# Moving seven-product operand preparation earlier in a Strassen feed-forward

## The chip, the cores and the metric

One NeuronCore of a Trainium2 chip runs the whole program. The metric is the device time of one execution in microseconds (us), lower is better.

## The reference, cut to what matters

The program computes a hybrid decoder in f32: two layers with a squared-ReLU feed-forward, then a block with a gated feed-forward. Only the three feed-forwards touch this change.

```python
def _mlp(x, w_up, w_down):                     # twice: DEPTH = 2, D_MODEL 1024, D_FF 4096, 512 tokens
    h = jax.nn.relu(x @ w_up)
    return (h * h) @ w_down
...
        gate = causal_dwconv3(h @ w_gate[i], ffn_conv_w[i], ffn_conv_b[i])      # D_FF_2 2816
        x = x + (jax.nn.silu(gate) * (h @ w_up[i])) @ w_down[i]
```

## The kernel before, in words

Every f32 matmul is done as three fp32r matmuls of 128x128 by 128x512 (`mm3`, L202 to L204): high by high, high by low, low by high. An operand is therefore split first: ScalarE (ACT) casts the high part (L119), VectorE (DVE) subtracts it to get the low part (L120). TensorE (PE) takes both.

**Up parts.** The hidden features are made in "parts" of 256 columns: two PSUM banks, 48 matmuls, two weight chunks (`wchunk`, or `pair_of` in the gated block) that are loaded by SP, then split on ACT and DVE into one of four `wh`/`wl` buffers. In the two MLPs a part is evacuated by ACT (ReLU, L1003, square, L1008). In the gated block a gate part `gp` goes through a convolution (L1310, L1311, L1313) and SiLU (L1582), and an up part `up` is multiplied in on DVE, into `hr` (L1592) or, for groups 8 to 10, into `a` (L1597) and split again into `ah`, `al`.

**Strassen steps.** The product with the down weights is done, for 1024 hidden columns at a time, as seven products of 24 matmuls each (`down_steps`, a generator that yields after each product). It runs three times per MLP and twice in the gated block (c = 0, 1). The feature side comes from two raw tiles `hr` with quarters A11, A21 (`ra`) and A12, A22 (`rb`). `a_op` copies a quarter into a split tile `aop` (one ACT cast, one DVE subtraction), `a_sum` (L910) forms a sum of quarters in place on DVE. The weight side comes from four tiles `wq`: `b_sum` (L916, DVE) and `b_op`. The products, with their feature operand: 1 a11; 2 s3 = A11 - A21; 3 s2 = A22 - A21'; 4 a12; 5 s1 = A11 + A22'; 6 a22, copied before A22 is overwritten; 7 s4 = A12 - A22'. `add` (L880) adds finished banks `r` into the residual on DVE.

**What sets the order.** A scheduler orders each engine's queue by the order in which the code is written, less a head start: operand and sum instructions have 120 places (`A_PRIO`), weight splits 80 or 60. Each engine then runs its queue strictly in that order. In the MLPs the mix is product 1, 2, 3, part, 4, part, 5, 6, part, 7, part (`WEAVE`); in the gated block one product and one part alternate, gate and up in turn, so that product 3 of c = 0 stands between the up part of group 4 and the gate part of group 5, and product 3 of c = 1 between the up part of group 8 and the gate part of group 9. There are 13 tiles for operands, features and inputs (`bp`) and 8 PSUM banks, of which the products hold up to six.

`tc.issue_after(ins)` orders, of the instructions written inside it, those on the engine of `ins` behind `ins` in that engine's queue.

Of the kernel before, what the change touches and what calls it, by code (L numbers as in the profile page):

```python
# [14 lines left out]
AF = mybir.ActivationFunctionType  # L15
ALU = mybir.AluOpType
# [30 lines left out]
A_PRIO, B_PRIO = 120, 80  # L47
# [4 lines left out]
def tile_hybrid_decoder(ctx: ExitStack, tc: tile.TileContext, io: dict, out: bass.AP):  # L52
    nc = tc.nc
# [9 lines left out]
    def pool(name, bufs, side=None):  # L63
        return tc.tile_pool(name=name, bufs=bufs, side=side, reuse_waits="tile")
# [3 lines left out]
    def big(name, dt=F32R):  # L68
        n_big[0] += 1
        return bp.tile([P, 4, S], dt, tag="b", name=f"{name}_{n_big[0]}")  # L70

    def bank(name="pb"):
        n_big[0] += 1
        return ps.tile([P, S], F32, tag="ps", name=f"{name}_{n_big[0]}")

    def small(n, name):
        n_big[0] += 1
        return sm.tile([P, n], F32, tag=f"s{n}", name=f"{name}_{n_big[0]}")
# [14 lines left out]
    turned = {}  # L93
# [24 lines left out]
    def split(hi, lo, src, src2=None):  # L118
        turned["hi"] = nc.scalar.copy(out=hi, in_=src).ins  # L119
        return nc.vector.tensor_tensor(out=lo, in0=src, in1=hi.bitcast(F32), op=ALU.subtract)  # L120
# [79 lines left out]
    def mm3(o, st, mv, start, stop):  # L200
        (sh, sl), (mh, ml) = st, mv
        nc.tensor.matmul(o, lhsT=sh, rhs=mh, start=start, stop=False, skip_group_check=True)  # L202
        nc.tensor.matmul(o, lhsT=sh, rhs=ml, start=False, stop=False, skip_group_check=True)  # L203
        nc.tensor.matmul(o, lhsT=sl, rhs=mh, start=False, stop=stop, skip_group_check=True)  # L204
# [43 lines left out]
    def krows(W, k0, kn, c0, n):  # L248
        return W[k0 * P:(k0 + kn) * P, c0:c0 + n].rearrange("(k p) c -> p k c", p=P)
# [203 lines left out]
    class Norm:  # L453
# [5 lines left out]
        def add(self, gi, t, pb, alpha):  # L459
            if t not in self.sums:  # L460
                self.sums[t] = small(2, "sum")
            cs = slice(gi * 512, gi * 512 + 512)
            nc.vector.scalar_tensor_tensor(out=self.x[:, t, cs], in0=self.x[:, t, cs], scalar=alpha, in1=pb,
                                           op0=ALU.mult, op1=ALU.add, accum_out=self.sums[t][:, gi:gi + 1])
# [412 lines left out]
    def ev_add(x, alpha):  # L877
        def ev(gi, t, pb):
            cs = slice(gi * 512, gi * 512 + 512)
            nc.vector.scalar_tensor_tensor(out=x[:, t, cs], in0=x[:, t, cs], scalar=alpha, in1=pb,  # L880
                                           op0=ALU.mult, op1=ALU.add)
        return ev
# [2 lines left out]

    ts2 = slice(0, 256), slice(256, 512)

    def down_steps(mb, wd, row, ra, rb, alpha):


        A11, A21, A12, A22 = ra[:, :, ts2[0]], ra[:, :, ts2[1]], rb[:, :, ts2[0]], rb[:, :, ts2[1]]
        B = {}
        for r, h in ((0, 0), (1, 1), (0, 1), (1, 0)):
            n_big[0] += 1
            B[r, h] = q = mb.tile([P, 4, S], F32, tag="q", name=f"wq_{n_big[0]}")
            for i in range(2):
                nc.sync.dma_start(out=q[:, 2 * i:2 * i + 2, :],
                                  in_=krows(wd, row + r * 4 + 2 * i, 2, h * 512, 512))
        B11, B12, B21, B22 = B[0, 0], B[0, 1], B[1, 0], B[1, 1]

        def a_op(src):
            o = big("aop")
            hl = o.rearrange("p k c -> p (k c)").rearrange("p (f k c) -> p f k c", f=2, k=4)
            with tc.high_priority(offset=A_PRIO):
                split(hl[:, 0], hl[:, 1], src)
            return hl

        def a_sum(out, a, b, op):
            with tc.high_priority(offset=A_PRIO):
                nc.vector.tensor_tensor(out=out, in0=a, in1=b, op=op)  # L910

        def b_sum(out, a, b, op):
            with tc.high_priority(offset=A_PRIO):
                for i in range(2):
                    ks = slice(2 * i, 2 * i + 2)
                    nc.vector.tensor_tensor(out=out[:, ks, :], in0=a[:, ks, :], in1=b[:, ks, :], op=op)  # L916

        def b_op(src):
            res = []
            for i in range(2):  # L920
                n_big[0] += 1
                wh = wp.tile([P, 1024], F32R, tag="wh", name=f"wh_{n_big[0]}")
                wl = wp.tile([P, 1024], F32R, tag="wl", name=f"wl_{n_big[0]}")
                with tc.high_priority(offset=B_PRIO):
                    split(wh, wl, src[:, 2 * i:2 * i + 2, :].rearrange("p k c -> p (k c)"))
                res.append([t.rearrange("p (k c) -> p k c", k=2) for t in (wh, wl)])
            return res

        def product(R, a, b, start):
            for i, (wh, wl) in enumerate(b):  # L930
                for tb in range(2):
                    for k in range(2):
                        ts_ = slice(tb * P, (tb + 1) * P)
                        kk = 2 * i + k
                        mm3(R[tb], (a[:, 0, kk, ts_], a[:, 1, kk, ts_]), (wh[:, k, :], wl[:, k, :]),
                            start and kk == 0, kk == 3)

        def add(R, th, h, al=1.0):
            for tb in range(2):
                ev_add(x, al)(h, 2 * th + tb, R[tb])  # L940

        def banks2(n):
            return [bank(n) for _ in range(2)]

        a11 = a_op(A11)
        b = b_op(B11)
        R1 = banks2("r")
        product(R1, a11, b, True)
        for th, h in ((0, 1), (1, 0), (1, 1)):
            add(R1, th, h, alpha)  # L950
        yield
        a_sum(A21, A11, A21, ALU.subtract)
        s3 = a_op(A21)
        b_sum(B12, B22, B12, ALU.subtract)
        b = b_op(B12)
        R3 = banks2("r")
        product(R3, s3, b, True)
        add(R3, 1, 1)
        yield
        a22 = a_op(A22)  # L960
        a_sum(A22, A22, A21, ALU.subtract)
        s2 = a_op(A22)
        b_sum(B11, B12, B11, ALU.add)
        b = b_op(B11)
        R2 = banks2("r")
        product(R2, s2, b, True)
        add(R2, 1, 0)
        yield
        a12 = a_op(A12)
        b = b_op(B21)  # L970
        product(R1, a12, b, False)
        add(R1, 0, 0, alpha)
        yield
        a_sum(A11, A11, A22, ALU.add)
        s1 = a_op(A11)
        b_sum(B21, B21, B11, ALU.subtract)
        b_sum(B11, B22, B11, ALU.subtract)
        b = b_op(B11)
        product(R2, s1, b, False)
        add(R2, 1, 1)  # L980
        yield
        b = b_op(B21)
        product(R3, a22, b, False)
        add(R3, 1, 0)
        yield
        a_sum(A12, A12, A22, ALU.subtract)
        s4 = a_op(A12)
        b = b_op(B22)
        product(R2, s4, b, False)
        add(R2, 0, 1)  # L990
        yield
# [316 lines left out]
    def conv3(y, u, wi, nm, m, bi):  # L1308

        nc.scalar.activation(y, u, AF.Identity, scale=col(wi + 2 * nm + m), bias=col(bi + m))  # L1310
        nc.vector.scalar_tensor_tensor(out=y[:, 1:], in0=u[:, :S - 1], scalar=col(wi + nm + m), in1=y[:, 1:],  # L1311
                                       op0=ALU.mult, op1=ALU.add)
        nc.vector.scalar_tensor_tensor(out=y[:, 2:], in0=u[:, :S - 2], scalar=col(wi + m), in1=y[:, 2:],  # L1313
                                       op0=ALU.mult, op1=ALU.add)
# [245 lines left out]
    wg, wu, wd = io["w_gate_2"][0], io["w_up_2"][0], io["w_down_2"][0]  # L1560
    with pool("ff", 2) as ff:
        H = []

        RAW = {}
# [12 lines left out]
        def gate_ev(gr, banks):  # L1577
            for m in range(2):
                n_big[0] += 1
                Y[gr, m] = y = ff.tile([P, S], F32, tag="y", name=f"y_{n_big[0]}")  # L1580
                conv3(y, banks[m], V_FW, 22, gr * 2 + m, V_FB)
                nc.scalar.activation(y, y, AF.Silu)  # L1582

        def up_ev(gr, banks):
            if gr < 8 and gr % 2 == 0:
# [58 lines left out]
                gated(gr, part)  # L1644
        with pool("fb", 4) as fb:
            for c in range(2):
                ds = down_steps(fb, wd, c * 8, RAW.pop(2 * c), RAW.pop(2 * c + 1), 1.0)
                for gr in range(4 * c + 4, min(4 * c + 8, 11)):
                    for part in range(2):
                        next(ds, None)  # L1650
                        gated(gr, part)
                for _ in ds:
                    pass
# [100 lines left out]
```

## Time and profile before

| what | value |
|---|---|
| time, median of 3 runs (lowest, highest) | 1725.74 us (1725.26, 1726.1) |
| the profiled execution's own time | 1721.95 us |
| its span, first to last instruction | 1720.2 us |
| PE busy, share of the span | 1679.5 us, 98% |
| DVE busy | 1109.6 us, 65% |
| ACT busy | 827.4 us, 48% |
| mean granted TensorE clock | 0.991 of full speed |

The profile is of one execution. A busy matmul of 389 ns overlaps the next one, so the pace of PE is read from the distance between starts. A timeline row gives start, length, engine, line, operation, output<-inputs, how many were merged, and in brackets the idle time before it with what ended it.

### The profile page before, as it was taken

Reading aid. Unit: us, or ns where it says so; the run is one execution under the profiler, and the core shown is the slowest. Engines: PE = TensorE matmul, PEld = TensorE weight load, DVE = VectorE, ACT = ScalarE, POOL = GpSimd, SP = SyncE. Lnnn points to the kernel's source line nnn. Section 1 sums busy time; section 2 is a strip of 40 time slices with the busy share of each in tenths; the row PEclk is TensorE's granted clock in tenths of the full one; section 3 lists DMA queues with packets and bytes.
Section 4 is the critical chain, followed back from the end, with each engine's and each line's share of the span. In section 5 each row is a group of like instructions: output and inputs, shape, how many; then the busy total and the mean of one; then the engine's idle time right before and its main releaser. Section 6 shows DMA issues by size and latency. Waiting matters only on the chain.

```text
span 1720.2 us, 21303 instructions
## 1 busy us (share of the span) xinstructions
PE 1679.5 (98%) x8239; PEld 1388.6 (81%) x8239; DVE 1109.6 (65%) x1938; ACT 827.4 (48%) x1415; POOL 8.0 (0%) x10
## 2 busy tenths in 40 slices
PE   8799999999999999999999999999999999999999
PEld 8577898888888877798888888988778878878887
DVE  5577558685845678747576846556765567667553
ACT  4366445444543578444444545444853333434442
POOL 0000000000000000000000000001000000000000
PEclk9899999999999999999999999999999999999999
DMA  5722442423132323413333133132352223321331
GB/s 183 107 66 79 142 147 62 134 74 123 49 111 86 105 69 113 158 50 98 98 98 98 49 128 107 40 132 86 100 183 62 86 86 92 117 63 60 99 97 62
DMA packets 128087, 167.57 MB, mean 97 GB/s; under 512 B 9049, under 2 KB 84082, under 8 KB 127986
## 3 DMA queue, kind: packets, MB, share of 16 engines
q1 hardware_dynamic: 119072, 150.03, 28.0%
q10 hardware_dynamic: 8914, 16.18, 3.9%
q8 instruction: 65, 1.06, 0.3%
q14 instruction: 36, 0.29, 0.1%
HBM read 160.95 MB, written 5.24 MB: 97 GB/s over the span
## 4 chain that ended last, share of the span: by engine, by line
PE 92%; DVE 3%; DMA 2%; ACT 2%; ACTq 1%; issue 0%; SPq 0%; DVEq 0%
PE up L203 8%; PE up L202 8%; PE up L204 8%; PE r L204 6%; PE r L202 6%; PE r L203 6%; PE tt L203 3%; PE tt L204 3%; PE tt L202 3%; PE tm L202 2%; PE tm L204 2%; PE fm L202 2%; PE tm L203 2%; PE fm L203 2%; PE fm L204 2%; PE gp L202 2%
## 5 line engine op out<-in xcount | busy, mean ns | idle before, releaser
L120 DVE TENSOR_TENSOR wl<-wr,wh 128x1024 fp32r<-128x1024 f32 (+5 forms) x219 | 223.0, 1031 | 183.0 <-ACT wh L119 182.2
L119 ACT CAST wh<-wr 128x1024 fp32r<-128x1024 f32 (+5 forms) x219 | 193.5, 898 | 285.2 <-PE up L203 112.5
L203 PE MATMUL up<-xtl,wh 128*128 128x512 f32 x608 | 236.5, 389 | 0.0
L202 PE MATMUL up<-xth,wh 128*128 128x512 f32 x608 | 236.5, 389 | 0.0
L204 PE MATMUL up<-xth,wl 128*128 128x512 f32 x608 | 236.2, 389 | 0.0
L120 DVE TENSOR_TENSOR wl<-wq,wh 128x1024 fp32r<-128x1024 f32 x112 | 136.8, 1222 | 109.5 <-ACT wh L119 109.5
L119 ACT CAST wh<-wq 128x1024 fp32r<-128x1024 f32 x112 | 118.1, 1054 | 172.4 <-PE r L204 94.0
L202 PE MATMUL r<-wh,aop 128*128 128x512 f32 x448 | 175.8, 392 | 6.2 <-ACT aop L119 6.2
L203 PE MATMUL r<-wl,aop 128*128 128x512 f32 x448 | 175.4, 392 | 0.0
L204 PE MATMUL r<-wh,aop 128*128 128x512 f32 x448 | 174.3, 395 | 0.0
L204 PEld LDWEIGHTS up<-xth,wl 128*128 128x128 f32 x608 | 114.1, 188 | 23.7
L203 PEld LDWEIGHTS up<-xtl,wh 128*128 128x128 f32 x608 | 114.1, 188 | 23.6
L202 PEld LDWEIGHTS up<-xth,wh 128*128 128x128 f32 x608 | 114.1, 188 | 23.6
L202 PEld LDWEIGHTS r<-wh,aop 128*128 128x128 f32 x448 | 84.8, 189 | 24.7 <-ACT aop L119 7.5
L204 PEld LDWEIGHTS r<-wh,aop 128*128 128x128 f32 x448 | 84.6, 189 | 21.6 <-DVE aop L120 4.2
L203 PEld LDWEIGHTS r<-wl,aop 128*128 128x128 f32 x448 | 84.7, 189 | 17.8
L880 DVE SCALAR_TENSOR_TENSOR x<-x,r 128x512 f32<-128x512 f32 x144 | 92.3, 681 | 1.2 <-PE r L204 1.2
L120 DVE TENSOR_TENSOR aop<-hr,aop 128x1024 fp32r<-128x1024 f32 x56 | 67.1, 1221 | 24.5 <-ACT aop L119 24.5
L916 DVE TENSOR_TENSOR wq<-wq,wq 128x1024 f32<-128x1024 f32 x64 | 76.3, 1219 | 5.2 <-DMA wq<-in_w_down_dram 4.1
L203 PE MATMUL gp<-xtl,wh 128*128 128x512 f32 x160 | 62.3, 389 | 0.0
L202 PE MATMUL gp<-xth,wh 128*128 128x512 f32 x160 | 62.3, 389 | 0.0
L204 PE MATMUL gp<-xth,wl 128*128 128x512 f32 x160 | 62.2, 389 | 0.0
(423 smaller groups left out, 3552.9 us busy)
## 6 DMA issues: line engine op xcount, KB each, us to landing
wr<-in_mlp_w_up_dram SPq DMA_DIRECT2D x64, 512.0 KB, 3.8
wq<-in_mlp_w_down_dram SPq DMA_DIRECT2D x48, 512.0 KB, 4.8
wr<-in_w_in_dram SPq DMA_DIRECT2D x24, 512.0 KB, 4.9
wr<-in_w_gate_dram SPq DMA_DIRECT2D x22, 512.0 KB, 3.6
wr<-in_w_up_dram SPq DMA_DIRECT2D x22, 512.0 KB, 3.7
wr<-in_mlp_w_down_dram SPq DMA_DIRECT2D x16, 512.0 KB, 3.8
wq<-in_w_down_dram SPq DMA_DIRECT2D x16, 512.0 KB, 4.0
wr<-in_mla_w_o_dram SPq DMA_DIRECT2D x8, 512.0 KB, 3.7
```

What stands on the lines that cost most here:

```text
L119: turned["hi"] = nc.scalar.copy(out=hi, in_=src).ins
L120: return nc.vector.tensor_tensor(out=lo, in0=src, in1=hi.bitcast(F32), op=ALU.subtract)
L202: nc.tensor.matmul(o, lhsT=sh, rhs=mh, start=start, stop=False, skip_group_check=True)
L203: nc.tensor.matmul(o, lhsT=sh, rhs=ml, start=False, stop=False, skip_group_check=True)
L204: nc.tensor.matmul(o, lhsT=sl, rhs=mh, start=False, stop=stop, skip_group_check=True)
L880: nc.vector.scalar_tensor_tensor(out=x[:, t, cs], in0=x[:, t, cs], scalar=alpha, in1=pb, op0=ALU.mult, op1=ALU.add)
L916: nc.vector.tensor_tensor(out=out[:, ks, :], in0=a[:, ks, :], in1=b[:, ks, :], op=op)
```

## The change

In `down_steps`, the sum and the split of a product's feature operand are written one product earlier: behind the matmuls of the product before and ahead of that product's `add` and `yield`, so ahead of the part that follows the `yield`. In the gated block the generator also gets the last SiLU instruction traced so far, and the `b_sum` instructions are written inside `tc.issue_after` of it. The diff:

```diff
-    def down_steps(mb, wd, row, ra, rb, alpha):
+    def down_steps(mb, wd, row, ra, rb, alpha, after=None):
...
         def b_sum(out, a, b, op):
-            with tc.high_priority(offset=A_PRIO):
+            with ExitStack() as es:
+                es.enter_context(tc.high_priority(offset=A_PRIO))
+                if after:
+                    es.enter_context(tc.issue_after(after))
...
         product(R1, a11, b, True)
+        a_sum(A21, A11, A21, ALU.subtract)
+        s3 = a_op(A21)
         for th, h in ((0, 1), (1, 0), (1, 1)):
             add(R1, th, h, alpha)
         yield
-        a_sum(A21, A11, A21, ALU.subtract)
-        s3 = a_op(A21)
...
         product(R3, s3, b, True)
-        add(R3, 1, 1)
-        yield
         a22 = a_op(A22)
         a_sum(A22, A22, A21, ALU.subtract)
         s2 = a_op(A22)
+        add(R3, 1, 1)
+        yield
...
         product(R2, s2, b, True)
+        a12 = a_op(A12)
         add(R2, 1, 0)
         yield
-        a12 = a_op(A12)
         b = b_op(B21)
         product(R1, a12, b, False)
+        a_sum(A11, A11, A22, ALU.add)
+        s1 = a_op(A11)
         add(R1, 0, 0, alpha)
         yield
-        a_sum(A11, A11, A22, ALU.add)
-        s1 = a_op(A11)
...
         product(R3, a22, b, False)
+        a_sum(A12, A12, A22, ALU.subtract)
+        s4 = a_op(A12)
         add(R3, 1, 0)
         yield
-        a_sum(A12, A12, A22, ALU.subtract)
-        s4 = a_op(A12)
...
-                nc.scalar.activation(y, y, AF.Silu)
+                turned["y"] = nc.scalar.activation(y, y, AF.Silu).ins
...
-                ds = down_steps(fb, wd, c * 8, RAW.pop(2 * c), RAW.pop(2 * c + 1), 1.0)
+                ds = down_steps(fb, wd, c * 8, RAW.pop(2 * c), RAW.pop(2 * c + 1), 1.0, turned["y"])
```

How the queues move, at three places. First ACT in the gated block, c = 0, from the up part of group 4 to product 3. `wh<-wr` is a weight chunk of a part, `wh<-wq` a weight split of a product, `aop` a feature operand. Before, the two operands of `hr_11775` for product 3 (a22, then s2) stand behind chunks of group 5:

```order
L119 CAST wh_12199<-wr_12198 128x1024
L119 CAST aop_12151<-hr_11775 128x1024
L119 CAST wh_12229<-wr_12228 128x1024
L119 CAST aop_12155<-hr_11775 128x1024
L119 CAST aop_12268<-hr_11775 128x1024
```

After, they stand between the weight splits of product 2, with the second chunk of group 4's gate part ahead and the first of its up part behind:

```order
L119 CAST wh_12009<-wr_12008 128x1024
L119 CAST aop_12084<-hr_11775 128x1024
L119 CAST wh_12050<-wq_11923 128x1024
L119 CAST aop_12088<-hr_11775 128x1024
L119 CAST wh_12054<-wq_11923 128x1024
L119 CAST wh_12096<-wr_12095 128x1024
```

So both moved up by one product and one part.

Second, DVE in the gated block, c = 1, at the end of the up part of group 8 (`a` evacuates its two banks). Before, from the first bank's evacuation on:

```order
L1597 TENSOR_TENSOR a_12989<-y_12873,up_12925 128x512
L120 TENSOR_TENSOR al_12988<-a_12989,ah_12987 128x512
L120 TENSOR_TENSOR aop_12997<-hr_12579,aop_12997 128x1024
L120 TENSOR_TENSOR wl_13076<-wr_13074,wh_13075 128x1024
L910 TENSOR_TENSOR hr_12579<-hr_12579,hr_12148 128x4x256
L1597 TENSOR_TENSOR a_12993<-y_12878,up_12926 128x512
```

After:

```order
L1600 TENSOR_TENSOR a_12996<-y_12877,up_12932 128x512
L120 TENSOR_TENSOR al_12995<-a_12996,ah_12994 128x512
L120 TENSOR_TENSOR aop_13040<-hr_12583,aop_13040 128x1024
L120 TENSOR_TENSOR aop_13150<-hr_12155,aop_13150 128x1024
L120 TENSOR_TENSOR wl_13079<-wr_13077,wh_13078 128x1024
L1600 TENSOR_TENSOR a_13000<-y_12882,up_12933 128x512
```

Ahead of the second bank's evacuation stood the low part of a22, a chunk and the sum for s2; now the low parts of a12 and s1 and the chunk.

Third, DVE in the first MLP, c = 0, from product 3's operand to the second chunk of the part behind it. Before:

```order
L120 TENSOR_TENSOR aop_2797<-hr_2319,aop_2797 128x1024
L120 TENSOR_TENSOR wl_2843<-wr_2841,wh_2842 128x1024
L880 SCALAR_TENSOR_TENSOR x_375_1795<-x_375_1795,r_2720 128x512
L880 SCALAR_TENSOR_TENSOR x_375_1795<-x_375_1795,r_2719 128x512
L880 SCALAR_TENSOR_TENSOR x_375_1795<-x_375_1795,r_2720 128x512
L880 SCALAR_TENSOR_TENSOR x_375_1795<-x_375_1795,r_2719 128x512
L880 SCALAR_TENSOR_TENSOR x_375_1795<-x_375_1795,r_2720 128x512
L120 TENSOR_TENSOR wl_2873<-wr_2871,wh_2872 128x1024
```

After:

```order
L120 TENSOR_TENSOR aop_2795<-hr_2319,aop_2795 128x1024
L120 TENSOR_TENSOR aop_2836<-hr_2319,aop_2836 128x1024
L120 TENSOR_TENSOR wl_2846<-wr_2844,wh_2845 128x1024
L880 SCALAR_TENSOR_TENSOR x_375_1795<-x_375_1795,r_2720 128x512
L880 SCALAR_TENSOR_TENSOR x_375_1795<-x_375_1795,r_2719 128x512
L880 SCALAR_TENSOR_TENSOR x_375_1795<-x_375_1795,r_2720 128x512
L880 SCALAR_TENSOR_TENSOR x_375_1795<-x_375_1795,r_2719 128x512
L880 SCALAR_TENSOR_TENSOR x_375_1795<-x_375_1795,r_2720 128x512
L910 TENSOR_TENSOR hr_2318<-hr_2318,hr_2319 128x4x256
L120 TENSOR_TENSOR wl_2876<-wr_2874,wh_2875 128x1024
```

The low part of a12 now stands ahead of the part's first chunk, and the sum for s1 ahead of its second. On SP and POOL every row stands where it stood. With the `issue_after` taken out of the changed kernel, all queues stay as they are with it.

## Rows read from the trace of the kernel before

**Rows 1.** The page: busy time, share of the span, instructions, by engine.
```profile
PE 1679.5 (98%) x8239; PEld 1388.6 (81%) x8239; DVE 1109.6 (65%) x1938; ACT 827.4 (48%) x1415; POOL 8.0 (0%) x10
```

**Rows 2.** Waits of PE, whole span: waiter, releaser, total us, times, longest.
```profile
PE r L202 <- ACT aop L119: 6.2, 2, 4.4
...
PE tm L202 <- ACT ptp L119: 0.6, 1, 0.6
```

**Rows 3.** Timeline of PE, gated block, c = 0, into product 3.
```profile
1416.69 0.39 PE L204 MATMUL up<-xth,wl 128*128 128x512 f32 x1
1418.93 0.50 PE L202 MATMUL r<-wh,aop 128*128 128x512 f32 x1 [1.86 <-ACT aop L119]
1419.27 0.39 PE L203 MATMUL r<-wl,aop 128*128 128x512 f32 x1
```

**Rows 4.** Windows: us, PE, PEld, DVE, ACT, POOL busy (instructions), granted clock, DMA, GB/s.
```profile
1384.00:1417.00 33.00, 33.00 (x146) 27.05 (x145) 20.56 (x24) 12.11 (x14) 0.00 (x0) 1.00 0.35 103
...
1419.00:1432.00 13.00, 13.00 (x57) 10.74 (x58) 12.47 (x13) 4.94 (x5) 0.00 (x0) 1.00 0.15 42
...
1548.70:1554.10 5.40, 5.35 (x12) 3.98 (x13) 5.40 (x6) 2.41 (x3) 0.00 (x0) 0.50 0.17 61
```

**Rows 5.** Timeline of all engines, gated block, c = 1, into product 3.
```profile
1542.93 1.05 ACT L119 CAST aop<-hr 128x1024 fp32r<-128x1024 f32 x1
...
1543.98 0.39 PE L204 MATMUL up<-xth,wl 128*128 128x512 f32 x1
1544.01 1.22 DVE L120 TENSOR_TENSOR aop<-hr,aop 128x1024 fp32r<-128x1024 f32 x1 [0.26 <-ACT aop L119]
...
1546.40 1.22 DVE L910 TENSOR_TENSOR hr<-hr,hr 128x1024 f32<-128x1024 f32 x1
...
1547.65 1.99 ACT L119 CAST aop<-hr 128x1024 fp32r<-128x1024 f32 x2 [2.43 <-DVE hr L910]
...
1548.75 0.79 PE L202 MATMUL r<-wh,aop 128*128 128x512 f32 x1 [4.38 <-ACT aop L119]
```

**Rows 6.** Timeline of DVE, gated block, c = 0, around product 1.
```profile
1384.48 0.69 DVE L1592 TENSOR_TENSOR hr<-y,up 128x512 f32<-128x512 f32 x1 [2.03 <-PE up L204]
1385.34 1.23 DVE L120 TENSOR_TENSOR wl<-wr,wh 128x1024 fp32r<-128x1024 f32 x1 [0.17 <-ACT wh L119]
```

**Rows 7.** Timeline of ACT, same place: second weight split of product 2.
```profile
1389.92 1.05 ACT L119 CAST wh<-wq 128x1024 fp32r<-128x1024 f32 x1 [1.67 <-PE r L204]
```

**Rows 8.** Timeline of PE, gated block, c = 1, in product 7.
```profile
1617.47 0.39 PE L203 MATMUL r<-wl,aop 128*128 128x512 f32 x1
1617.85 0.50 PE L204 MATMUL r<-wh,aop 128*128 128x512 f32 x1
1618.19 0.39 PE L202 MATMUL r<-wh,aop 128*128 128x512 f32 x1
```

**Rows 9.** Waits of the weight loads in the first MLP, 270 to 512 us.
```profile
PEld r L204 <- DVE aop L120: 1.7, 5, 0.4
```

**Rows 10.** Timeline of PE, first MLP, c = 0, in product 4.
```profile
297.01 0.39 PE L203 MATMUL r<-wl,aop 128*128 128x512 f32 x1
297.33 0.50 PE L204 MATMUL r<-wh,aop 128*128 128x512 f32 x1
297.67 0.40 PE L202 MATMUL r<-wh,aop 128*128 128x512 f32 x1
```

**Rows 11.** First MLP, c = 0: DVE behind product 3's operand, then PE's first part.
```profile
278.71 1.22 DVE L120 TENSOR_TENSOR wl<-wr,wh 128x1024 fp32r<-128x1024 f32 x1
...
282.83 1.22 DVE L120 TENSOR_TENSOR wl<-wr,wh 128x1024 fp32r<-128x1024 f32 x1
...
285.45 0.39 PE L202 MATMUL up<-xth,wh 128*128 128x512 f32 x1
```

**Rows 12.** The tile aop: instructions, duration in ns (min/median/max), first and last start.
```profile
L119 ACT CAST aop<-hr x56: 1032/1048/1057, 256.9 to 1615.5; 128x1024 fp32r<-128x1024 f32 x56
L120 DVE TENSOR_TENSOR aop<-hr,aop x56: 1216/1220/1227, 258.0 to 1616.6; 128x1024 fp32r<-128x1024 f32 x56
```

## The prediction, made before the changed kernel was run

> **What bounds the kernel now.** I read the busy times first. PE is busy for 98% of the span, DVE for 65%, ACT for 48% [rows 1], so time can only be won where PE stands still or runs below its pace. Its pace is in a window without a stop: 146 matmuls in 33.00 us, 0.226 us each, at granted clock 1.00, which is 2.4 GHz [rows 4]. The waits of PE come next. Of its named waits, one group belongs to the edited code: products `r` waiting for the ACT cast of `aop`, 6.2 us in two stops, the longest 4.4 us [rows 2]. Both stops lie in the gated block. The timeline puts the first ahead of product 3 of c = 0 [rows 3] and the second ahead of product 3 of c = 1 [rows 5]. The operand is s2, the only one that needs a copy, a sum and another copy in a row.
>
> Why it is late is in [rows 5]. a22 is cast at 1542.93 while PE does its last up matmuls. Its low part runs on DVE from 1544.01, the sum for s2 starts only at 1546.40, the ACT cast of s2 waits 2.43 us for that sum and starts at 1547.65, and PE starts at 1548.75. The whole chain was asked for too late; no engine in it is overloaded.
>
> **The change part by part.**
>
> *Product 3's operand, c = 0.* PE's starts are 1416.69, 1418.93 and 1419.27 [rows 3]. The stop is 1418.93 - 1416.69 - 0.23 = 2.0 us, and the next distance is 0.34, so 0.1 more: 2.1 us. The order of ACT puts both casts one product and one part earlier, between the weight splits of product 2. There the second half of `hr` is there at 1384.48 + 0.69 = 1385.2 [rows 6]; ACT can cast a22 until about 1386.4; DVE is on a chunk until 1386.6 [rows 6], then does the low part and the sum, 1.22 us each [rows 5, 12], until 1389.0; ACT casts s2 until 1390.1, and the low part is there by about 1392.1, with a weight split and one addition ahead of it. Product 3 is due at 1416.9, so some 25 us are in hand, and the 2.1 us go. The price is on ACT: the second weight split of product 2 started at 1389.92 [rows 7] and would start at 1390.1. It is not used before about 1403 (product 2 starts a part after product 1, 48 x 0.226 = 10.8 us, and needs it after 12 matmuls). That costs nothing.
>
> *Product 3's operand, c = 1.* The stop is 1548.75 - 1543.98 - 0.23 = 4.5 us [rows 5]. Behind it the clock reads 0.50, or 1.2 GHz, and 12 matmuls take 5.40 us in place of 12 x 0.226 = 2.71 [rows 4]: 2.7 us more. The order moves this operand in the same way, so both go: 7.2 us. The clock fell after PE had stood still for 4.5 us; after the 2.0 us stop of c = 0 the next window reads 1.00 [rows 4].
>
> The Trainium skill's page "TensorE: Matmul & The Clock Gate" (What's actually happening) says that the monitor behind this clock runs free of the kernel, so that the point of a change varies from run to run. The trace shows one execution and can't tell. By that rule the timed runs may have paid no clock term at c = 1, which leaves 8.9 us to gain, or one at c = 0 as well, which makes it 14.3 us. I keep both as ends of the range and take the trace's case; the ends also follow without the page, since one stop lost the clock and one did not.
>
> *Product 7's operand, c = 1.* Two distances of 0.38 and 0.34 us [rows 8] in place of 0.23 each make 0.3 us; s4 now stands a part earlier, so this goes.
>
> *The MLPs.* Here a12 and s4, the operands of products 4 and 7, come late by their low part: five weight loads of the first MLP wait for it [rows 9], and the second MLP has an identical row. At the first of these PE's distances are 0.32 and 0.34 [rows 10], so 0.2 us is lost; ten such places make 2.0 us at most. The order after has these operands a part earlier, so I take all of it; the lower bound is 0, should other low parts then come late. What pays is DVE ahead of a part's chunks: one low part before the first chunk, and a sum more before the second. By [rows 11] the first chunk's low part would start at 278.71 + 1.22 = 279.9 and end at 281.2, due at 285.45; the second's would start at 282.83 + 2.44 = 285.3 and end at 286.5, due 24 matmuls after 285.45, at 290.9. Over 4 us are in hand each time, so I put it at nothing.
>
> *What is next late.* With product 3 of c = 1 on time at 1544.2, the gate part of group 9 starts at 1544.2 + 24 x 0.226 = 1549.6. It needs the PSUM banks of group 8's up part, since products hold the other six. Ahead of the second bank's evacuation DVE now does the low parts of a12 and s1 and one chunk: from 1544.01, where a22's low part ran [rows 5], 3 x 1.22 and 0.69 end at 1548.4. That is 1.2 us in time, the smallest margin I find. It costs nothing unless DVE slips by more.
>
> *The tie of the weight sums.* The instruction passed in is a SiLU, on ACT. The tie orders only instructions of that engine, and `b_sum` issues on DVE alone. The order of the changed kernel is the same with and without it: this part does nothing. Time 0, no bounds needed.
>
> Nothing is added or removed: same casts, sums, products and DMAs, and SP and POOL keep their order. The SP queue, which holds the chunk loads, follows when PE frees buffers, only sooner.
>
> **Sum.** 2.1 + 7.2 + 0.3 + 2.0 = 11.6 us, all on PE, which is the path. Against the profiled execution: 1721.95 - 11.6 = 1710.4 us. The runs' median lies 3.8 us above that execution for a reason that the trace doesn't show; the stops come from queue order, so I take the same 11.6 from 1725.74: 1714.1 us. The 0.6 us wait for `ptp` [rows 2] stays.
>
> **Rivals.**
>
> *A smaller gain.* The banks of group 8 come late after all, or the MLP's 2.0 us stay because the matmuls now want their low parts at once (in the order after, high and low products alternate from the start). A slip of 3 us on DVE would make PE wait 3.0 - 1.2 = 1.8 us. With both, 1714.1 + 1.8 + 2.0 = 1717.9; with the clock term not paid in the timed runs, 1720.6. For it: the margin is small. Against: the chain is counted with full durations, 1.22 us each, where DVE starts back-to-back ones closer together.
>
> *No change.* The stops repeat at the same step, and the operands would be held back by space and not by order: a cast can't start before one of the 13 tiles is free, so asking earlier moves nothing: 1725.7. That is the rule of the Trainium skill's "Perfetto Trace Analysis" (Optimization Strategy), that a gap which keeps coming back on the engine that should be full can mean that SBUF or PSUM has no room for the next tile. Against it: the cast of s2 waited for a DVE sum [rows 5], not for PE to let go of a tile, and I count at most 12 tiles at that place (four of input, two raw, two of `ah` and `al`, and a22, s2, a12, s1).
>
> *Slower.* The DVE work moved ahead of the parts in the MLPs. It happens six times, between products 3 and 4. If the second chunk's low part came more than 4.4 us later than I worked out, PE would wait at each, and every us beyond costs 6 us. From 11.6 / 6 = 1.9 us beyond the margin the gain is used up; at 3 us beyond it, 1714.1 + 18 = 1732. For it: six additions of the residual stand in the same stretch of DVE. Against: it takes over 7 us of delay in a stretch that moves by 2.44 us.
>
> *The change not doing what it says* is settled for the tie (nothing) and excluded for the operands by the order.
>
> **How the numbers follow.** A measurement of this kernel can tell about 0.2%, 3.5 us. Forecast, 1714.1: 0.74, with ends 1711.4 (a clock term at both stops; 1711.0 with 0.4 us of run spread) and 1716.8 (none). Smaller gain, 1717 to 1721: 0.14. No change: 0.07. Slower, 1732: 0.05. Faster is the first two, 0.88. The range goes from 1711 to 1719: the upper end is the forecast with no clock term (2.7) and without the MLP's 2.0, 1718.8, which leaves out the worse half of the second case and the last two.
>
> **What the profile after would show.** Right: no wait of `r` for `aop` on PE; product 3 of c = 0 and 1 starting 0.23 us after the up part's last matmul; clock 1.00 through both; no distances of 0.32 and 0.34 us in products 4 and 7 of the MLPs; the operand casts between the weight splits of product 2. Wrong: a wait of `gp` at group 9 for DVE's `a`, a wait of `up` for `wl` behind product 3 in the MLPs, or a cast of `aop` ended by PE.

## The result, and the profile after

| | before | after |
|---|---|---|
| time, median of 4 runs (lowest, highest) | 1725.92 us (1725.26, 1726.42) | 1714.83 us (1711.39, 1716.28) |
| ratio of the two, 95% interval | | 0.9933 (0.9916 to 0.995) |
| the profiled execution's own time | 1721.95 us | 1716.02 us |
| its span | 1720.2 us | 1714.1 us |
| mean granted TensorE clock | 0.991 | 0.991 |

The change is faster by 11.1 us, with an interval of 8.6 to 14.5 us; 11.6 were forecast. The two profiled executions lie only 5.9 us apart, and most of this section is about why. Busy times first, of the page after, as in [rows 1] (PEld is TensorE loading weights): the counts are those of before, and the busy times agree to 0.3%.

```profile
PE 1679.2 (98%) x8239; PEld 1392.8 (81%) x8239; DVE 1109.6 (65%) x1938; ACT 828.2 (48%) x1415; POOL 8.0 (0%) x10
```

The waits of PE from 1290 to 1660 us, after. The first group of [rows 2], `r` for `aop`, is gone; the 0.6 us for `ptp` stayed as forecast. The 3.3 us for `rv` stood there before, too; an experiment below comes back to it.

```profile
PE pt L447 <- DVE rv L422: 3.3, 1, 3.3
PE gt L202 <- ACT xth L119: 1.0, 1, 1.0
PE tm L202 <- ACT ptp L119: 0.6, 1, 0.6
```

The row for `rv` of the kernel before:

```profile
PE pt L447 <- DVE rv L422: 3.3, 1, 3.3
```

The timeline of PE after, at three places: product 4 of the first MLP (answers [rows 10]), product 3 of c = 0 ([rows 3]) and of c = 1 ([rows 5]).

```profile
301.64 0.39 PE L203 MATMUL r<-wl,aop 128*128 128x512 f32 x1
301.87 0.39 PE L204 MATMUL r<-wh,aop 128*128 128x512 f32 x1
302.10 0.39 PE L202 MATMUL r<-wh,aop 128*128 128x512 f32 x1
...
1420.43 0.39 PE L204 MATMUL up<-xth,wl 128*128 128x512 f32 x1
1420.66 0.39 PE L202 MATMUL r<-wh,aop 128*128 128x512 f32 x1
1420.89 0.39 PE L203 MATMUL r<-wl,aop 128*128 128x512 f32 x1
...
1545.56 0.39 PE L204 MATMUL up<-xth,wl 128*128 128x512 f32 x1
1545.78 0.39 PE L202 MATMUL r<-wh,aop 128*128 128x512 f32 x1
1546.01 0.39 PE L203 MATMUL r<-wl,aop 128*128 128x512 f32 x1
```

Every distance is 0.23 us. The windows after, columns as in [rows 4]. The first two rows are places that the change doesn't touch; the last three cover the stretches of [rows 4], at clock 1.00 throughout:

```profile
60.00:104.00 44.00, 27.75 (x103) 20.58 (x102) 26.12 (x63) 18.01 (x39) 0.00 (x0) 0.73 0.65 102
1285.00:1312.00 27.00, 22.69 (x152) 21.25 (x151) 18.62 (x31) 10.28 (x20) 0.00 (x0) 0.87 0.12 39
1384.00:1417.00 33.00, 33.00 (x147) 27.36 (x146) 23.95 (x27) 13.70 (x16) 0.00 (x0) 1.00 0.31 96
1417.00:1432.00 15.00, 15.00 (x68) 12.39 (x67) 13.76 (x15) 5.71 (x7) 0.00 (x0) 1.00 0.25 71
1540.00:1560.00 20.00, 20.00 (x90) 16.58 (x89) 16.86 (x18) 8.64 (x10) 0.00 (x0) 1.00 0.18 53
```

The same two untouched windows of the kernel before:

```profile
60.00:104.00 44.00, 28.18 (x121) 21.39 (x120) 28.77 (x75) 20.75 (x46) 0.00 (x0) 0.81 0.63 99
...
1285.00:1312.00 27.00, 23.41 (x175) 22.12 (x174) 18.73 (x32) 11.54 (x20) 0.00 (x0) 0.94 0.19 60
```

With the same order of instructions, this execution of the changed kernel got less clock there. To take that apart from the change, I compared the start of every n-th matmul in both traces (each holds 8239). The table gives how much longer each stage took than in the profile of before, in us, for this kernel and for the experiments below. *tie 1* and *tie 2* are two profiles of one kernel. Stages are named by their time before; a number in bold is the long form of the stage from 25 to 102 us, or what the binding tie of the experiments does.

| stage | after | s2_only | rest_only | half | notie | tie 1 | tie 2 | load3 |
|---|---|---|---|---|---|---|---|---|
| 0 to 25 | +1.5 | +1.9 | +1.1 | +0.1 | +0.8 | +2.0 | +0.5 | +1.1 |
| 25 to 102 | **+3.7** | **+3.7** | +0.3 | +0.1 | **+3.5** | **+3.6** | +0.1 | 0.0 |
| MLP 1 | -1.26 | -0.11 | -1.26 | -0.15 | -1.26 | -1.26 | -1.26 | -1.26 |
| 724 to 758 | -0.8 | +1.8 | -0.9 | -0.9 | +1.5 | -0.7 | -0.6 | -0.8 |
| MLP 2 | -1.25 | -0.10 | -1.25 | -0.07 | -1.25 | -1.25 | -1.25 | -1.25 |
| 1271 to 1308 | +2.0 | -0.2 | +1.7 | +2.0 | +0.9 | **-4.1** | **-4.1** | -0.1 |
| product 3, c = 0 | -2.17 | -2.17 | +1.60 | -2.17 | -2.17 | -2.17 | -2.17 | -2.17 |
| product 3, c = 1 | -7.28 | -7.28 | +0.28 | -7.19 | -7.28 | -7.28 | -7.28 | -7.15 |
| product 7, c = 1 | -0.32 | -0.03 | -0.32 | -0.02 | -0.32 | -0.32 | -0.32 | -0.32 |
| all else | -0.1 | -0.1 | -0.4 | +0.1 | 0.0 | 0.0 | 0.0 | -0.1 |
| sum | -6.0 | -2.7 | +0.9 | -8.2 | -5.6 | -11.4 | -16.3 | -12.0 |

In the five edited stages the changed kernel wins 1.26 + 1.25 + 2.17 + 7.28 + 0.32 = 12.3 us, and it does so to 0.01 us in three more profiles that hold the whole change. The other stages took 6.3 us more in this one execution. From 25 to 102 us the executions profiled here come in one of two forms, some 3.5 us apart, and the profile of before has the short one; the two profiles of one kernel, tie 1 and tie 2, have one each, so it is not the edit that chooses.

### The profile page after: what moved, and what is told of

Same layout as the page of the kernel before. It is cut to its first block, busy times and chain, and to the rows that moved or that the text cites. A ratio compares the mean times of both kernels' runs of the same rounds, so it can differ in the third digit from the quotient of the medians.

```text
span 1714.1 us, 21289 instructions
## 1 busy us (share of the span) xinstructions
PE 1679.2 (98%) x8239; PEld 1392.8 (81%) x8239; DVE 1109.6 (65%) x1938; ACT 828.2 (48%) x1415; POOL 8.0 (0%) x10
## 4 chain that ended last, share of the span: by engine, by line
PE 91%; DMA 3%; DVE 3%; ACT 2%; ACTq 1%; issue 1%; SPq 0%; DVEq 0%
PE up L203 8%; PE up L202 8%; PE up L204 8%; PE r L202 6%; PE r L203 6%; PE r L204 6%; PE tt L203 3%; PE tt L204 3%; PE tt L202 3%; PE tm L202 2%; PE tm L204 2%; PE tm L203 2%; PE fm L202 2%; PE fm L203 2%; PE fm L204 2%; PE gp L203 2%
```

## The experiments

Each was timed beside the kernel before on its own chip; before had a median of 1725.02 us (14 runs, 1722.08 to 1730.74) for the first four kernels and 1724.77 us (9 runs, 1721.86 to 1725.9) for the others.

| kernel | median (range, runs) | ratio to before, 95% |
|---|---|---|
| s2_only | 1714.95 (1713.88 to 1719.56, 5) | 0.9943 (0.9922 to 0.9964) |
| rest_only | 1721.05 (1717.99 to 1727.53, 10) | 0.9978 (0.9962 to 0.9994) |
| half | 1714.84 (1713.75 to 1717.92, 4) | 0.994 (0.9917 to 0.9964) |
| dve_tie (tie 1) | 1709.48 (1707.28 to 1712.66, 4) | 0.9906 (0.9876 to 0.9936) |
| notie | 1712.66 (1711.87 to 1716.4, 5) | 0.9935 (0.9922 to 0.9949) |
| tie_again (tie 2) | 1709.66 (1705.65 to 1710.27, 4) | 0.991 (0.9896 to 0.9924) |
| load3 | 1710.0 (1 run) | |
| load6 | 1723.6 (1 run) | |

**Product 3's operand alone.** Against the kernel before:

```diff
         product(R3, s3, b, True)
-        add(R3, 1, 1)
-        yield
         a22 = a_op(A22)
         a_sum(A22, A22, A21, ALU.subtract)
         s2 = a_op(A22)
+        add(R3, 1, 1)
+        yield
```

> The kernel before, with one operand group alone moved: a22, the sum for s2 and s2 itself are written ahead of product 3's predecessor's add and yield; s3, a12, s1 and s4 stay where they were, and there is no tie. Theory (queue order, each place pays for itself): both stops in front of product 3 of the gated block go (2.1 us at c = 0, 7.2 us at c = 1 with the half clock behind it), the 0.3 us in product 7 and the 0.2 us places in the MLPs stay. In the records: no wait of r for aop on PE, weight loads in the MLPs still waiting for aop. Time: before minus 9.3, about 1716.5 us. Rival, that the operands are held up by space for tiles: the stops stay and the time is that of the kernel before, about 1725.8. Rival, that the gain comes from the MLPs, whose ten places hide more than the records show: the time falls by under 5 us.

1714.95 us, 10.1 under before, for 9.3 expected. In its profile both stops are gone (-2.17 and -7.28), and the small places stay; the waits of the weight loads in its first MLP are those of [rows 9] to 0.1 us:

```profile
PEld r L204 <- DVE aop L120: 1.7, 5, 0.3
```

The number of tiles is that of the kernel before, so space did not hold the operand: order alone moved it.

**Everything but product 3's operand.** Against the changed kernel, the reverse of that edit:

```diff
         product(R3, s3, b, True)
+        add(R3, 1, 1)
+        yield
         a22 = a_op(A22)
         a_sum(A22, A22, A21, ALU.subtract)
         s2 = a_op(A22)
-        add(R3, 1, 1)
-        yield
```

> The changed kernel with product 3's operand (a22, its sum, s2) put back behind the add and the yield; s3, a12, s1 and s4 stay early. Theory (each place pays for itself): two stops of about 2.0 and 4.5 us in front of product 3 of the gated block, the second with a granted clock near 0.50 behind it, and only the small places gone, 2.5 us in the MLPs (by the records of the changed kernel) and 0.3 us in product 7. Time: before minus 2.8, about 1723 us. Rival, that the earlier a12 and s1 alone already free the DVE and ACT queues in front of product 3: the stops shrink and the time falls below 1720. Rival, that the MLPs hold the larger share: below 1720 with both stops whole.

1721.05 us, 4.0 under before, with an interval of 1.0 to 6.6 us: it holds the 2.8 expected. By the stages the two parts add up to the whole: 9.45 us (s2_only) and 2.83 (rest_only, without the two stops) are 12.28. The medians, 10.1 and 4.0 against 11.1 for the whole, are not exact enough to show that. The stops are whole, by the waits of PE in its trace:

```profile
PE r L202 <- ACT aop L119: 6.2, 2, 4.4
```

One thing was not expected. The stop at c = 0 is as long as before (1.85 us of wait, 1.86 in [rows 3]), but the stage took 1.60 us longer, since here the clock fell behind it. Windows of rest_only behind the stop, then behind that of c = 1:

```profile
1417.50:1420.00 2.50, 1.76 (x6) 1.47 (x7) 2.50 (x3) 2.50 (x3) 0.00 (x0) 0.85 0.00 0
1420.00:1425.00 5.00, 5.00 (x18) 3.96 (x18) 3.06 (x3) 0.98 (x2) 0.00 (x0) 0.74 0.14 20
1425.00:1430.00 5.00, 5.00 (x24) 4.14 (x23) 4.82 (x6) 1.20 (x2) 0.00 (x0) 1.00 0.25 88
1550.00:1555.40 5.40, 5.40 (x13) 3.98 (x13) 5.40 (x6) 2.10 (x4) 0.00 (x0) 0.50 0.11 37
```

18 matmuls took 5.00 us where 22 fit at full pace. In [rows 4] that stretch read 1.00. So a 2.0 us stop cost a clock term in one profile and none in the other. A term at c = 0 is one of the two ends that the prediction kept, at 1.6 us here in place of the 2.7 that it took. The other end, no term behind the stop of c = 1, shows in no profile: both that have this stop read 0.50 there.

**Two of the three steps early.** Against the kernel before: a22 and the sum for s2 early, the copy of s2 where it was.

```diff
+        a22 = a_op(A22)
+        a_sum(A22, A22, A21, ALU.subtract)
         add(R3, 1, 1)
         yield
-        a22 = a_op(A22)
-        a_sum(A22, A22, A21, ALU.subtract)
         s2 = a_op(A22)
```

> The kernel before, with a22 and the sum for s2 moved early as in the changed kernel, but s2's own split left behind the add and the yield. It tells whether the stop is the three-step chain (copy, sum, copy) or only the last copy. Theory (the chain): with two of the three steps done a product and a part early, ACT can cast s2 as soon as the queue reaches it, so the stop of c = 0 goes whole and that of c = 1 whole or to under 0.6 us (the low part, used by the third matmul), the clock is not lost, and the time is within 1 us of product 3's operand moved whole, about 1716.5 to 1717.5. Rival, that the late place of the last cast in the ACT queue is what makes PE wait: stops of 1 us and more stay at both places, and the time stays above 1720.

1714.84 us, the same as with all three steps moved (s2_only, 1714.95). Its timeline at c = 1, ACT, PE and the weight loads:

```profile
1541.94 2.00 ACT L119 CAST aop<-hr 128x1024 fp32r<-128x1024 f32 x2
...
1543.22 0.40 PE L202 MATMUL r<-wh,aop 128*128 128x512 f32 x1
...
1544.30 0.19 PEld L204 LDWEIGHTS r<-wh,aop 128*128 128x128 f32 x1 [0.18 <-DVE aop L120]
```

The cast no longer waits for a sum (2.43 us in [rows 5]) and ends in time; the low part makes one weight load wait 0.18 us, and the stage loses 0.09 us to the whole change. So the late place of the last copy cost next to nothing; what cost 9.4 us was the copy and the sum ahead of it, asked for at the same point. Whether the first copy alone, moved early, would have done is not tested.

**A tie that binds.** Against the changed kernel: `turned` holds the last DVE instruction of the gate's convolution in place of the SiLU on ACT. For this `conv3` returns its last instruction, an edit that is not printed here. Its partner on the second chip, notie, is the changed kernel without the argument. tie_again is this kernel once more.

```diff
...
-                conv3(y, banks[m], V_FW, 22, gr * 2 + m, V_FB)
-                turned["y"] = nc.scalar.activation(y, y, AF.Silu).ins
+                turned["y"] = conv3(y, banks[m], V_FW, 22, gr * 2 + m, V_FB).ins
+                nc.scalar.activation(y, y, AF.Silu)
```

> The changed kernel with the tie made to bind: the instruction passed in is the last one of the convolution of the gate part, on DVE, in place of the SiLU, on ACT. The weight sums are DVE instructions, so now they are held. The first pair of sums, which in the changed kernel stands inside the chain of the norm ahead of the gated block (two times 1.22 us at 1286.9 and 1288.1), moves behind the convolution of the last gate part ahead of product 1. Theory (the sums delay the norm, and PE waits for the norm with its clock down): PE starts the gated block about 2.4 us earlier, and the time is 2 to 5 us under the changed kernel's, about 1710 to 1713. Rival 1 (the first x tiles of the norm, or the loads, set that start): the time is the changed kernel's, about 1715. Rival 2 (the held sums make the weight splits of product 1 late): PE waits for wh in front of product 1 and the time is longer than the changed kernel's by that wait.

> The changed kernel without the tie of the weight sums: the generator gets no instruction, and every engine's queue is the same as in the changed kernel. Theory (the tie as written orders nothing, since it names an instruction of ACT and the sums are on DVE): the time is that of the changed kernel, 1714.8 us, to within the run spread of about 3 us, and the two sums at the head of the gated block stand at the same place inside the chain of the norm. Rival (the tie adds a wait that the queues don't show): a difference of more than 3.5 us. It is also the partner of the binding tie on the same chip: by the first run of that, 1709.5, this one should be 4 to 6 us longer.

> The binding tie once more, in more rounds and beside the changed kernel without a tie. Theory (two weight sums of 1.22 us each in the chain of the norm hold PE back at the head of the gated block, and the clock falls there): 1709.5 us again, 4 to 6 us under the kernel without the tie, with the granted clock of 1285 to 1312 us near 1.00 against 0.87 there. Rival (the first four timed runs were lucky in the clock of earlier stages, where the time varies by up to 5 us): within 2 us of the kernel without the tie.

notie ran at 1712.66 us and won the same 12.3 us in the edited stages: the tie as written does nothing. The binding tie ran at 1709.48 and 1709.66 us, the first half a us under the 1710 to 1713 expected. Beside notie on one chip it is 3.0 us less by the medians, which is under the 4 to 6 expected, and 5.0 by the means (1708.8 against 1713.8, four and five runs); its highest run, 1710.27, lies under the lowest of notie, 1711.87. The place is plain in the stage table: all that it adds stands in 1271 to 1308, -4.1 twice, where the seven profiles without it have -0.2 to +2.0 (that of before is the zero). What it takes away is in the DVE timeline of notie, in the norm ahead of the gated block:

```profile
1288.41 0.14 DVE L422 TENSOR_SCALAR rv<-ss 128x1 f32<-128x1 f32 x1
1288.47 1.22 DVE L919 TENSOR_TENSOR wq<-wq,wq 128x1024 f32<-128x1024 f32 x1
1289.60 0.16 DVE L423 RECIPROCAL rr<-rv 128x1 f32<-128x1 f32 x1
1289.67 1.21 DVE L919 TENSOR_TENSOR wq<-wq,wq 128x1024 f32<-128x1024 f32 x1
...
1292.65 0.21 DVE L426 SCALAR_TENSOR_TENSOR ra<-rv,rs 128x1 f32<-128x1 f32 x1
...
1290.06 1.03 PE L447 MATMUL pt<-ident,xn 128*128 128x128 f32 x8
1294.43 1.97 PE L447 MATMUL pt<-ident,xn 128*128 128x128 f32 x8 [3.34 <-DVE rv L422]
...
1296.49 0.58 PE L202 MATMUL gt<-xth,awh 128*128 128x256 f32 x1
```

Two weight sums (`wq`) stand between the small steps of the norm, and behind them other work comes first; from `rv` to `ra` it takes 4.24 us, and PE, which needs the normed tile, stands for 3.34 us. In tie_again, from `rv` on, then PE:

```profile
1282.66 0.14 DVE L422 TENSOR_SCALAR rv<-ss 128x1 f32<-128x1 f32 x1
1282.84 0.16 DVE L423 RECIPROCAL rr<-rv 128x1 f32<-128x1 f32 x1
1283.33 0.22 DVE L426 SCALAR_TENSOR_TENSOR ra<-rv,rs 128x1 f32<-128x1 f32 x1 [0.33 <-ACT rs L424]
...
1284.31 1.91 PE L447 MATMUL pt<-ident,xn 128*128 128x128 f32 x16
1286.56 0.38 PE L202 MATMUL gt<-xth,awh 128*128 128x256 f32 x1 [0.34 <-ACT xth L119]
1287.57 0.39 PE L203 MATMUL gt<-xtl,awh 128*128 128x256 f32 x1 [0.63 <-DVE xtl L120]
```

0.67 us from `rv` to `ra`, 0.34 and 0.63 us of waiting, and the first feed-forward matmul (`gt`) 2.3 us after the transposes began (1284.31 to 1286.56) in place of 6.4 (1290.06 to 1296.49). The clock keeps its level as well; the window of tie_again, to set beside 0.87 and 0.94 above:

```profile
1285.00:1312.00 27.00, 26.03 (x217) 25.51 (x215) 17.69 (x29) 14.52 (x23) 0.00 (x0) 1.00 0.25 79
```

In neither profile of the tie does PE wait for the weights of a product, which was the rival. This kernel is the fastest found: faster than the one before and, going by notie, than the changed one.

**The margins.** Against the changed kernel, three DVE instructions behind a12 that leave the values as they are (six in load6):

```diff
         a12 = a_op(A12)
+        for _ in range(3):
+            a_sum(A12, A12, A12, ALU.max)
         add(R2, 1, 0)
```

> The changed kernel with three more DVE instructions of 128x1024, 1.22 us each, behind the copy of a12 in every Strassen step; they leave the values as they are. In the MLPs they stand between the two chunks of the part behind product 3; in the gated block at c = 1 two of them stand ahead of the evacuation of group 8's second bank. It tests the two margins of the prediction. Theory: in the MLPs 4.6 us were in hand (low part of the second chunk at 291.4, due at 296.0), three cost 3.7, so PE makes no stop there; at group 9 about 1.5 us were in hand and 2.4 are added, so the gate part waits about 1 us for DVE, once. Time: the changed kernel's plus 1. Rival (the MLP margin was smaller than worked out): six stops of over 0.5 us behind product 3, plus 3 us or more.

> The same with six more DVE instructions of 1.22 us, 7.3 us in all, between the two chunks of the part in the MLPs; at group 9 two stand ahead of the evacuation as with three. Theory (the margin of 4.6 us and the price of the rival that ends slower): the second chunk comes 7.3 - 4.6 = 2.7 us late at each of the six places, so PE makes six stops of about 2.7 us there, 16 us, and the time is 16 us and more over the changed kernel's (more where the clock falls behind a stop), about 1730 to 1740. Rival (the scheduler or the queues absorb it): stops of under 1 us, less than 6 us in all.

load3: no stop in the MLPs, as expected, but no stop of PE at group 9 either, where 1 us was expected. Its 1710.0 us, one run, lie 4.8 us under the changed kernel's median, not 1 us above it; the table shows why: its profile has the short form from 25 to 102 us, and the edited stages are those of the changed kernel to 0.13 us. Its timeline at group 9; `hr<-hr` is added work, `a<-y,up` the evacuation of group 8's second bank:

```profile
1544.06 1.22 DVE L910 TENSOR_TENSOR hr<-hr 128x1024 f32<-128x1024 f32 x1
...
1545.14 0.39 PE L202 MATMUL gp<-xth,wh 128*128 128x512 f32 x1
1545.19 0.68 DVE L1602 TENSOR_TENSOR a<-y,up 128x512 f32<-128x512 f32 x1
...
1545.60 0.51 PEld L202 LDWEIGHTS gp<-xth,wh 128*128 128x128 f32 x2
...
1545.82 0.62 PE L202 MATMUL gp<-xth,wh 128*128 128x512 f32 x2
```

The evacuation ends at 1545.87, after the first of the two merged matmuls began at 1545.82; so the second bank of `gp` begins with the second of them, at 1546.05, four matmuls behind the first bank. Its weight load is held up by some 0.1 us (two such loads take 0.42 us at full pace, here 0.51), and the stretch is 0.13 us longer than in the changed kernel: the margin is just used up. In the changed kernel itself:

```profile
1549.00 0.68 DVE L1600 TENSOR_TENSOR a<-y,up 128x512 f32<-128x512 f32 x1
...
1551.22 0.39 PE L202 MATMUL gp<-xth,wh 128*128 128x512 f32 x1
...
1551.90 0.39 PE L202 MATMUL gp<-xth,wh 128*128 128x512 f32 x1
```

The evacuation ended at 1549.68 and the second bank was wanted at 1551.90: 2.2 us in hand, where I had counted 1.5 to the first bank.

load6: stops come where they were expected, and at places where they were not, by PE's waits in its first MLP (the second MLP has an identical row):

```profile
PE up L204 <- DVE wl L120: 3.1, 5, 0.8
```

By the stage comparison the two MLPs take 10.2 us more than in the changed kernel, for 16 expected. The six places behind product 3 cost 1.1 us each, 6.5 us in all, and not 2.7 each; the other 3.7 us are four stops of 0.9 us in the parts behind product 4, which nobody had counted. Two things in the trace go the way of the smaller price, though no run parts them: six DVE instructions of 1.22 us that start 1.13 us apart take 6.8 us and not 7.3, and the scheduler put two product matmuls ahead of the waiting one in PE's queue, 0.45 us. Against load3, with the same clock in the early stages, the span is 13.6 us longer; the remaining 3.4 us lie outside the MLPs and were not followed up. The time, 1723.6 us in one run, is 8.8 us over the changed kernel's median and under the 1730 to 1740 expected. The mechanism holds; at the places for which it was priced, the price was too high by more than twice.

## Why the prediction was right

*Product 3, c = 0.* 2.1 us by the sum, 2.17 measured. The queue of ACT after, at product 2:

```profile
1388.95 1.04 ACT L119 CAST aop<-hr 128x1024 fp32r<-128x1024 f32 x1
1390.94 1.06 ACT L119 CAST wh<-wq 128x1024 fp32r<-128x1024 f32 x1 [0.94 <-PE r L204]
1392.74 1.05 ACT L119 CAST aop<-hr 128x1024 fp32r<-128x1024 f32 x1 [0.74 <-DVE hr L910]
1393.69 1.05 ACT L119 CAST wh<-wq 128x1024 fp32r<-128x1024 f32 x1
```

By the stage table this execution is 3.75 us behind that of before here (the sum of its rows down to 1271 to 1308, the first matmul's 0.1 included). Less that, a22 ends at 1386.2 (forecast 1386.4), s2 at 1390.0 (1390.1), and the second split starts at 1389.9 (1390.1). The three-step chain was followed rightly.

*Product 3, c = 1.* 7.2 by the sum, 7.28 measured, and the clock stayed at 1.00, so the clock term was rightly in it. That no such term stood at c = 0 holds for the execution that was read; rest_only shows that another can have one.

*Product 7.* 0.3, measured 0.32.

*The MLPs.* This term was mis-sized: 2.0 us by the sum, 2.51 measured, 0.25 at each of ten places. I had counted the two long distances, 0.32 and 0.34; behind them some eight more of 0.23 to 0.24 follow in the trace of before, which [rows 10] cut off. The next row there shows the first, 0.24 behind 297.67:

```profile
297.91 0.40 PE L203 MATMUL r<-wl,aop 128*128 128x512 f32 x1
```

The margin was right: the second chunk's low part, forecast 286.5 in the time of before, ended at 291.42 in a trace that is 5.1 us behind, so at 286.3:

```profile
290.20 1.22 DVE L120 TENSOR_TENSOR wl<-wr,wh 128x1024 fp32r<-128x1024 f32 x1
```

*What is next late.* No wait at group 9, as forecast. The margin was put at 1.2 us and was 2.2, since the gate part's second bank is first used three matmuls (0.7 us) behind the first and the evacuation ended 0.3 us sooner than counted, with back-to-back DVE instructions closer together.

*The tie.* It does nothing as written, as forecast: notie. That the sums which it is meant for cost 4 us at the head of the gated block is something I didn't look for; their row is DVE's and the wait of 3.3 us for `rv` was in the answer from which [rows 2] is taken.

*From the profile to the median.* The prediction took the same 11.6 us from 1725.74 as from the profiled execution. Against the medians that was right: 11.1 us in the first runs, 12.1 in those of notie. That the median came within 0.7 us of the forecast is in part luck, since the four runs spread over 4.9 us. Against the one profiled execution it failed: 1710.4 us were forecast and 1716.02 measured, with the mechanism whole. Profiles of other executions with the whole change ran at 1716.40 (notie) and, with a little work added, 1710.0 us (load3). The step that failed is the silent one that stages not edited take the same time in any execution. The reason for the 3.8 us between before's profile and its median was left open; the stage table points to it, since that profile has the short form of 25 to 102 us. The timed runs left no records, so this is not shown for them.

*The rivals.* No change, by space for tiles: excluded by s2_only, which moved both stops with the same tiles; the Trainium skill's page "Perfetto Trace Analysis" (Optimization Strategy) says that a gap which keeps coming back on the engine that should be full can mean too little SBUF or PSUM for the next tile. Here that was not the cause. A smaller gain: group 9 did not wait, and the MLP's low parts came in time. Slower: its mechanism is real, as load6 shows, but it takes more than the 3.4 us of extra DVE work of load3.

## What to carry to other kernels

An operand that takes a copy, a sum and a copy on two engines is asked for with the whole chain in view; moving the first two steps was worth as much as all three. A tie orders only within the queue of the engine that it names, so its first question is on which engine the tied instruction runs; and early work is not free where it lands inside a chain of small steps that PE waits for. Compare two traces stage by stage, by the number of the matmul, before reading anything from two spans: here 6 us of 12 were hidden by stages that no one had edited, more than half of it where the granted clock was lower.

## What the runs showed of the hardware that was not expected

The granted clock behind a stop of one length differed between two kernels whose matmuls have the same order there: 1.00 in [rows 4] and 0.74 in rest_only, behind waits of 1.86 and 1.85 us. From 60 to 104 us it read 0.81 in six of the ten profiles of this case (before among them) and 0.73 in four, with nothing between, worth 3.5 us of a span. The Trainium skill's page "TensorE: Matmul & The Clock Gate" (What's actually happening) says that the monitor runs free of the kernel and that the point of change varies with it; these runs agree that it varies, and do not show why in two forms. And DVE instructions of 1.22 us that follow each other start 1.13 us apart (two `wq` sums and the small steps in notie, `aop` at 2.36 us for two after), so a queue of them is about 7% shorter than the sum of its durations.
